# Zero-padded heads: score products of 64-column heads made 128 rows deep, and zero rows in DRAM written later

## Chip, cores and metric

The kernel runs on one core of one Trainium2 chip, in one launch. The metric is the time of one execution in microseconds on the device. The core has TensorE (PE in the rows; PEld is its weight load), VectorE (DVE), ScalarE (ACT), GpSimd (POOL) and SyncE (SP, which here only issues transfers).

## What is computed

Two blocks of a transformer on 512 tokens of width 1024, all in float32. The parts that the change touches are three attentions whose heads have 64 columns:

```python
# block 1, second attention (8 heads of 64, the selected keys only)
s = jnp.einsum('bqhd,bqkhd->bhqk', qi, k_sel) * (DSA_HEAD_DIM ** -0.5)
p = jax.nn.softmax(jnp.where(sel_ok[:, None], s, NEG), axis=-1)
# block 2, stick-breaking attention (8 heads of 64)
z = jnp.einsum('bhqd,bhkd->bhqk', q_blk, k) * dh ** -0.5
log_keep = jnp.where(past, jax.nn.log_sigmoid(-z), 0.0)
between = lax.cumsum(log_keep, axis=3, reverse=True) - log_keep
a = jnp.where(past, jnp.exp(jax.nn.log_sigmoid(z) + between), 0.0)
# block 2, dilated mixture (12 heads of 64 in three groups, dilations 1, 4, 16)
s = jnp.einsum('brhnqd,brhnkd->brhnqk', qs, kc) * dh ** -0.5
```

Between them stand a first attention in block 1 with 96 columns a head, a mixture of 32 experts, a memory attention with 128 columns a head in block 2, and at the end a layer that gathers rows of two tables of 16,384 experts.

## The kernel before

Every float32 product is made of three: each operand is split into a high part (a rounded copy, fp32r) and a low part (what is left), and `mm3` (lines 178 to 180) adds high x high, high x low and low x high into one PSUM bank. `split` (lines 185 and 187, or 188 and 189 with a scale) makes the parts: ScalarE casts the high one, VectorE (or GpSimd, where a weight is split for it) subtracts for the low one. Weights come in units of up to 512 KB through a ring of buffers `wr` and are split into `wh` and `wl`.

The block starts with the norm of four tiles of 128 tokens (`norm_T`): ScalarE sums squares, VectorE makes the root (`rs_v`, `rs_t`, `rs_y`) and the scaled tile `ny`, TensorE transposes it (line 271) and `split` writes it into HT and LT. Then the projection with `w1a` in four units, whose products (128x360) need all of that, and the next one with `w1b`. In this place GpSimd also zeroes a tile `zr` and writes it to DRAM with eight transfers: seven into `xs`, where the expert stage scatters tokens to later, and one into the last rows of `ys`.

A score product takes the features of one head from the rows of a tile: two heads of 64 columns stand above one another in 128 rows, and the product slices 64 of them (`rows`, `bs`). Between these products TensorE does other work, to keep it busy while the other engines do softmax: `fill` steps, products of the gates and output projections with 128 rows, transpositions of probabilities, and products with the values. A scheduler sets the order of the instructions on each engine from the program's dependencies and its own estimates, so code in another place or with other dependencies moves rows elsewhere.

In the stick-breaking stage each step (`logits`) copies scores z to u, makes az on VectorE, ScalarE, ScalarE, VectorE and GpSimd, and splits it into sp; `weights`, two steps later, adds products of sp with a triangle and makes the weights `at`. There are three buffers for az and four for u. In the dilated stage a step makes three products: s1 with 512 columns and two with 128.

The products of the memory attention (`mkT`, `mqT`) and of the index scores (`kiT`, already zero-padded per head) have 128 rows; those of the first attention (`kT`, `qT`) have 96.

Of the kernel before, what the change touches and what calls it, by code (L numbers as in the profile page):

```python
# [145 lines left out]
class Kernel:  # L146
# [233 lines left out]
    def block1_mix(self, cx, cm):  # L380
        nc, a = self.nc, self.a
        with ExitStack() as c0:
# [30 lines left out]
            with ExitStack() as c2:  # L413
# [29 lines left out]
                zr = pi.tile([P, XW // 7], F32, name="zr")  # L443
                nc.gpsimd.memset(zr, 0.0)
                for g in range(1, 8):
                    nc.gpsimd.dma_start(self.xs[g * P:(g + 1) * P].rearrange("p (r n) -> p r n", r=7),
                                      zr[:, None, :].to_broadcast([P, 7, XW // 7]))
                nc.gpsimd.dma_start(self.ys[896:1024].rearrange("p (r n) -> p r n", r=8),
                                  zr[:, None, 0:D // 8].to_broadcast([P, 8, D // 8]))
# [78 lines left out]
            with ExitStack() as c2:  # L528
# [31 lines left out]
            with ExitStack() as c2:  # L560
                pd = self.pool(c2, "b1d")
                qbT = [pd.tile([P, 4, 512], F32R, name=f"qbT{i}") for i in range(2)]
                kbT = [pd.tile([P, 4, 512], F32R, name=f"kbT{i}") for i in range(2)]
                vb = [pd.tile([P, NT, 512], F32R, name=f"vb{i}") for i in range(2)]
                hv = lambda x: x.rearrange("p (h r) -> p h r", h=8)
                for j, (dst, scale) in enumerate(((qbT, 0.125), (kbT, None))):
# [7 lines left out]
                    for jj in range(4):  # L574
                        self.transp([tok[:, t, jj * P:(jj + 1) * P] for t in range(NT)], P, dst[0][:, jj], dst[1][:, jj],
                                    scale=scale)
# [628 lines left out]
    def stick_qk(self, HT, LT, pool, half):  # L1205
        qT = [pool.tile([P, 2, 512], F32R, name=f"sqT{i}", tag=f"sqT{i}", bufs=1) for i in range(2)]
        kT = [pool.tile([P, 2, 512], F32R, name=f"skT{i}", tag=f"skT{i}", bufs=1) for i in range(2)]
# [10 lines left out]
    def stick(self, HT, LT, pq, qk, oT, fill):  # L1218

        nc = self.nc  # L1220
        with ExitStack() as c:
            pk = self.pool(c, "b2s")
            qT, kT = qk
            neg = pk.tile([P, P], F32, name="neg")
# [5 lines left out]
            nc.vector.tensor_copy(tri[1], neg)  # L1230
            self.tc.keep_in_program_order(nc.scalar.preload_act_table_set("natural_log_exp_and_others"))
            for half in range(2):
# [4 lines left out]
                self.stick_heads(pk, qT, kT, v, tri, oT[:, 2 * half:2 * half + 2], fill, half)  # L1237

    def stick_heads(self, pk, qT, kT, v, tri, oT, fill, half):
        nc = self.nc  # L1240
        sp, at = {}, {}

        def logits(i):
# [624 lines left out]
```

## Time and profile before

| | us |
|---|---|
| median of 3 runs | 2795.93 |
| lowest, highest | 2793.38, 2797.89 |
| the profiled execution | 2794.61 |
| its span, first to last instruction | 2792.6 |
| TensorE busy | 2674.3 (96%) |
| VectorE, ScalarE, GpSimd busy | 2066.8, 1290.4, 767.4 |

The granted clock of TensorE was 0.985 of full speed in the mean. Busy time of TensorE is from start to modelled end, so durations of neighbours overlap; how long a product holds the engine is read from the start of the next one. A row of the order of time gives start, duration, engine, line and operands; `64*128 64x256` is a stationary tile of 64 rows and 128 columns and a moving one of 64 rows and 256 columns. In brackets stands how long the engine had been idle, and what ended that.

### The profile page before, as it was taken

To read this page: it belongs to the slowest core of one execution; us is meant where nothing else is said; L and a number is where in the kernel's file an instruction comes from. 1 tells how busy PE (TensorE), PEld (TensorE's weight loads), DVE (VectorE), ACT (ScalarE), POOL (GpSimd) and SP (SyncE) were. 2 spreads that over 40 slices of the span, in tenths; PEclk is the share of its full clock that TensorE was granted. 3 is DMA by queue.
4 is the path that set the end of the run, shared out by engine and by line. 5 is a ranking of instruction groups with operands and counts; after the bars stand their busy time and mean duration, and the time that the engine had idled before them with its cause. 6 is when DMAs were issued, how large, how long until landed. Compare 5 with 4: busy or idle time off the path is not lost. (4 is left out here: it accounts for less than half of the span.)

```text
span 2792.6 us, 38328 instructions
## 1 busy us (share of the span) xinstructions
PE 2674.3 (96%) x13674; PEld 2296.3 (82%) x13674; DVE 2066.8 (74%) x4037; ACT 1290.4 (46%) x2029; POOL 767.4 (27%) x530
## 2 busy tenths in 40 slices
PE   6999999899999999899998999999999999999999
PEld 5887777677777878798877898999988888888887
DVE  4758856699988464654574898988778888778887
ACT  3544443577766564643433233355653333333332
POOL 1121110000001232210213351210125666665662
PEclk9999999999999999899999999999999999999999
DMA  7222228599984332231533246777678999999996
GB/s 190 78 69 80 83 84 300 197 344 354 355 306 125 110 106 85 72 98 61 170 132 134 77 139 196 229 252 255 247 281 317 342 355 357 348 347 338 347 338 231
DMA packets 231381, 595.69 MB, mean 213 GB/s; under 512 B 26128, under 2 KB 94992, under 8 KB 229520
## 3 DMA queue, kind: packets, MB, share of 16 engines
q1 hardware_dynamic: 192016, 450.52, 46.8%
q0 software_dynamic: 39168, 142.65, 14.4%
q8 instruction: 110, 1.80, 0.3%
q14 instruction: 87, 0.71, 0.1%
HBM read 524.91 MB, written 68.19 MB: 212 GB/s over the span
## 5 line engine op out<-in xcount | busy, mean ns | idle before, releaser
L185 ACT CAST wh<-wr 128x1024 fp32r<-128x1024 f32 (+3 forms) x637 | 621.4, 991 | 564.0 <-PE acc L179 226.9
L187 DVE TENSOR_TENSOR wl<-wr,wh 128x1024 fp32r<-128x1024 f32 (+3 forms) x483 | 574.7, 1204 | 143.1 <-ACT wh L185 141.7
L187 POOL TENSOR_TENSOR wl<-wr,wh 128x1024 fp32r<-128x1024 f32 (+1 forms) x154 | 318.9, 2080 | 777.1 <-ACT wh L185 738.3
L1576 POOL DMA_INDIRECT wr<-in_peer_u,idx x128 | 174.9, 1366 | 445.0 <-DVE dot L1581 204.8
L180 PE MATMUL acc<-hp,wl 128*128 128x384 f32 (+1 forms) x816 | 287.7, 353 | 7.6 <-DVE wl L187 7.6
L178 PE MATMUL acc<-hp,wh 128*128 128x384 f32 (+1 forms) x816 | 286.4, 352 | 0.0
L179 PE MATMUL acc<-hp,wh 128*128 128x384 f32 (+1 forms) x816 | 285.3, 350 | 0.0
L1576 POOL DMA_INDIRECT wr<-in_peer_v,idx x128 | 186.1, 1454 | 154.6 <-DVE x L1579 66.4
L185 ACT CAST WH<-act 128x384 fp32r<-128x384 f32 x128 | 65.9, 515 | 321.5 <-PE s L179 312.7
L1579 DVE SCALAR_TENSOR_TENSOR x<-wr,dot,x 128x1024 f32<-128x1024 f32 x128 | 195.2, 1525 | 18.2 <-DMA wr<-in_peer_v,idx 17.4
L1581 DVE CUSTOM_DVE_ANT_0 hy<-wr,gbc 128x1024 f32<-128x1024 f32 x128 | 173.0, 1352 | 39.9 <-DMA wr<-in_peer_u,idx 39.3
L178 PE MATMUL acc<-wh,WH 128*128 128x512 f32 x512 | 198.4, 392 | 3.9 <-ACT WH L185 3.9
L179 PE MATMUL acc<-wl,WH 128*128 128x512 f32 x512 | 200.9, 392 | 0.8 <-DVE wl L187 0.6
L180 PE MATMUL acc<-wh,WL 128*128 128x512 f32 x512 | 198.6, 389 | 0.0
L180 PEld LDWEIGHTS acc<-hp,wl 128*128 128x128 f32 x816 | 154.6, 190 | 16.2 <-DVE wl L187 11.1
L179 PEld LDWEIGHTS acc<-hp,wh 128*128 128x128 f32 x816 | 154.4, 189 | 5.3
L178 PEld LDWEIGHTS acc<-hp,wh 128*128 128x128 f32 x816 | 154.7, 190 | 4.8
L178 PEld LDWEIGHTS acc<-wh,WH 128*128 128x128 f32 x512 | 96.6, 189 | 23.0 <-ACT WH L185 4.2
L179 PEld LDWEIGHTS acc<-wl,WH 128*128 128x128 f32 x512 | 96.7, 189 | 20.9 <-DVE wl L187 2.4
L180 PEld LDWEIGHTS acc<-wh,WL 128*128 128x128 f32 x512 | 96.3, 188 | 20.3
L179 PE MATMUL s<-wl,XT 128*128 128x512 f32 x256 | 104.6, 409 | 5.4 <-DVE wl L187 5.3
L187 DVE TENSOR_TENSOR WL<-act,WH 128x384 fp32r<-128x384 f32 x128 | 78.0, 611 | 42.7 <-ACT WH L185 42.3
(650 smaller groups left out, 6885.7 us busy)
## 6 DMA issues: line engine op xcount, KB each, us to landing
wr<-in_peer_vL SPq DMA_DIRECT2D x128, 512.0 KB, 6.1
wr<-in_peer_uT SPq DMA_DIRECT2D x126, 512.0 KB, 4.8
wr<-in_w_gu SPq DMA_DIRECT2D x122, 512.0 KB, 5.3
wr<-in_w_dn SPq DMA_DIRECT2D x62, 512.0 KB, 5.3
gd<-stg SPq DMA_DIRECT2D x12, 2048.0 KB, 8.7
G<-gd SPq DMA_DIRECT2D x32, 768.0 KB, 11.2
act<-ad SPq DMA_DIRECT2D x72, 192.0 KB, 7.9
ad<-act SPq DMA_DIRECT2D x70, 192.0 KB, 4.1
```

Of the source, the lines that this page charges most:

```text
L178: mm(out, lh, rh, start=start, stop=False)
L179: mm(out, lh, rl, start=False, stop=False)
L180: return mm(out, ll, rh, start=False, stop=stop)
L185: nc.scalar.copy(H, src)
L187: return (le or nc.vector).tensor_tensor(L, src, H.bitcast(F32), op=ALU.subtract)
L1576: nc.gpsimd.indirect_dma_start(out=row, out_offset=None, in_=a["peer_u" if f == "dot" else "peer_v"], in_offset=bass.IndirectOffsetOnAxis( ...
L1579: nc.vector.scalar_tensor_tensor(x[:, 0], row, dot0[:, e:e + 1], x[:, 0], op0=ALU.mult, op1=ALU.add)
L1581: nc.vector.tensor_tensor_reduce(scr, row, h0, 1.0, 0.0, ALU.mult, ALU.add, accum_out=dot0[:, e:e + 1])
```

## The change

Four edits. The zero writes to `xs` and `ys` move from the first projection to the start of the first attention, behind the last weights fetched until then. In the second attention the keys are kept whole as float32 in `kb`, and `qk(h)` splits the 64 rows of one head into its half of `kbT`, a tile whose other rows are zero; there are two, for even and odd heads. The queries keep both heads in 128 rows, and the zero rows take the other head's part out. The stick-breaking stage does the same with `sk` and `skT` (`keys(h)`), and has two buffers for az in place of three. In the dilated stage it is the queries that are padded: `qT` holds them whole, and `queries(i)` splits 64 rows x 3 groups x 128 for a step into one of four tiles `dq`.

```diff
-                zr = pi.tile([P, XW // 7], F32, name="zr")
-                nc.gpsimd.memset(zr, 0.0)
-                for g in range(1, 8):
-                    nc.gpsimd.dma_start(self.xs[g * P:(g + 1) * P].rearrange("p (r n) -> p r n", r=7),
...
+                zr = pa.tile([P, XW // 7], F32, name="zr")
+                nc.gpsimd.memset(zr, 0.0)
+                rows = [(self.xs[g * P:(g + 1) * P], 7, XW // 7) for g in range(1, 8)] + [(self.ys[896:1024], 8, D // 8)]
+                for dst, r, n in rows:
+                    d = nc.gpsimd.dma_start(dst.rearrange("p (r n) -> p r n", r=r), zr[:, None, 0:n].to_broadcast([P, r, n]))
+                    self.after(d, self.loaded, "behind the weights")
...
-                kbT = [pd.tile([P, 4, 512], F32R, name=f"kbT{i}") for i in range(2)]
+                kb = pd.tile([P, 4, 512], F32, name="kb")
+                kbT = self.heads(pd, "kbT", 1)
...
+                            for t in range(NT):
+                                self.T(pt[:, t * P:(t + 1) * P], src[t])
+                            nc.scalar.copy(kb[:, jj], pt)
...
                 def qk(h):
-                    bs = slice((h % 2) * 64, (h % 2) * 64 + 64)
-                    return [x[bs, h // 2] for x in qbT], [x[bs, h // 2] for x in kbT]
+                    r = slice(64 * (h % 2), 64 * (h % 2) + 64)
+                    self.split(*[x[r, h % 2] for x in kbT], kb[r, h // 2])
+                    return [x[:, h // 2] for x in qbT], [x[:, h % 2] for x in kbT]
...
-                self.split(kT[0][:, cc - 2], kT[1][:, cc - 2], ps)
+                self.nc.scalar.copy(kT[:, cc - 2], ps)
...
+            kp = self.heads(pk, "skT", 1)
...
+        def keys(h):
+            r = slice(64 * (h % 2), 64 * (h % 2) + 64)
+            self.split(*[x[r, h % 2] for x in kp], kT[r, h // 2])
+
+        keys(0)
...
+            if i % NT == 1 and h < 3:
+                keys(h + 1)
...
-            ins = self.mm3(z[:, :n], kT[0][rows, h // 2, ks], kT[1][rows, h // 2, ks], qT[0][rows, h // 2, qs],
-                           qT[1][rows, h // 2, qs], True, True)
+            ins = self.mm3(z[:, :n], kp[0][:, h % 2, ks], kp[1][:, h % 2, ks], qT[0][:, h // 2, qs], qT[1][:, h // 2, qs],
+                           True, True)
...
-            az = pk.tile([P, 512], F32, name="az", tag="az", bufs=3)
+            az = pk.tile([P, 512], F32, name="az", tag="az", bufs=2)
...
+                def queries(i):
+                    hh, r = i // 4, i % 4
+                    rows = slice(64 * hh, 64 * hh + 64)
+                    self.split(*[x[rows] for x in qp[hh][r % 2]], qT[rows, :, r * P:(r + 1) * P])
...
+                    if i < 7:
+                        queries(i + 1)
+                    q = lambda g: [x[:, g] for x in qp[hh][r % 2]]
+                    k = lambda g, s: [x[:, g, s] for x in kT]
...
+    def heads(self, pool, name, n):
+
+        K = [pool.tile([P, 2 * n, 512], F32R, name=f"{name}{i}", tag=f"{name}{i}", bufs=1) for i in range(2)]
+        for x in K:
+            v = x.rearrange("p (n h) t -> p n h t", h=2).bitcast(F32)
+            self.nc.gpsimd.memset(v[64:128, :, 0], 0.0)
+            self.nc.gpsimd.memset(v[0:64, :, 1], 0.0)
+        return K
```

GpSimd's order from the end of the zero fills at the start to the splits for the first attention (`wl` are low parts of the gates' weights, `kT` the rotated key columns of the first attention), before:

```order
L426 MEMSET pe_243 128x4x64
L444 MEMSET zr 128x147
L446 DMA xs<-zr 896x1x147 x7
L448 DMA ys<-zr 1024x1x128
L187 TENSOR_TENSOR wl<-wr,wh 128x1024 x3
L533 CAST kT_1360<-peT_237 32x512
```

and with the change, in the same place:

```order
L426 MEMSET pe_243 128x4x64
L187 TENSOR_TENSOR wl<-wr,wh 128x1024 x3
L526 CAST kT_1350<-peT_237 32x512
L526 CAST kT_1351<-peT_238 32x512
L526 CAST kT_1352<-peT_237 32x512
L526 CAST kT_1353<-peT_238 32x512
L529 MEMSET zr 128x147
L532 DMA xs<-zr 896x1x147 x7
L532 DMA ys<-zr 1024x1x128
L187 TENSOR_TENSOR wl<-wr,wh 128x1024 x9
```

The zero writes stand behind three weight splits and the four key copies now, and ahead of the weight splits for the rest of that attention.

ScalarE's order around the keys of the second attention (`t` is the bank with the transposed keys, `vb` the values), before:

```order
L185 CAST kbT_2770<-t 128x512 x2
L185 CAST wh<-wr 128x1024
L185 CAST kbT_2770<-t 128x512 x2
L185 CAST oaH<-oaT 128x512 x4
L185 CAST wh<-wr 128x1024
L185 CAST vb_2772<-acc 128x512 x4
L185 CAST wh<-wr 128x1024
```

and with the change, on ScalarE in the same place (`kb` holds the whole keys):

```order
L583 COPY kb<-t 128x512 x2
L185 CAST kbT_2771<-kb 64x512 x2
L185 CAST wh<-wr 128x1024
L583 COPY kb<-t 128x512 x2
L185 CAST oaH<-oaT 128x512 x4
L185 CAST wh<-wr 128x1024
L185 CAST vb_2777<-acc 128x512 x4
L185 CAST wh<-wr 128x1024
```

The whole keys are copied in the same place, and the first two heads are split there; the other six casts of 64x512 stand further down, one among the softmaxes of each head.

TensorE's order where the stick-breaking stage begins (`mPT` and `Pr` belong to the memory attention, `wh,HTb` with 256 columns to the projection of the values `sv`), before:

```order
L271 MATMUL t<-ident,Pr 128x128 x2
L178 MATMUL s<-sqT_9304,skT_9306 128x128
L179 MATMUL s<-sqT_9305,skT_9306 128x128
L180 MATMUL s<-sqT_9304,skT_9307 128x128
L178 MATMUL s<-sqT_9304,skT_9306 128x256
L179 MATMUL s<-sqT_9305,skT_9306 128x256
L180 MATMUL s<-sqT_9304,skT_9307 128x256
L271 MATMUL t<-ident,Pr 128x128 x2
L178 MATMUL acc<-mPT_9923,mv_9035 128x512
L178 MATMUL acc<-wh,HTb 128x256
L179 MATMUL acc<-wl,HTb 128x256
```

and with the change, behind that projection (`oH,wh` is a fill product):

```order
L178 MATMUL acc<-wh,HTb 128x256
L179 MATMUL acc<-wl,HTb 128x256
L180 MATMUL acc<-wh,LTb 128x256
L178 MATMUL s<-sqT_9321,skT_10107 128x128
L179 MATMUL s<-sqT_9322,skT_10107 128x128
L180 MATMUL s<-sqT_9321,skT_10108 128x128
L178 MATMUL acc<-oH,wh 128x512
L179 MATMUL acc<-oH,wh 128x512
L180 MATMUL acc<-oH,wl 128x512
L178 MATMUL acc<-oH,wh 128x512
L179 MATMUL acc<-oH,wh 128x512
L180 MATMUL acc<-oH,wl 128x512
```

The first two score products of the stage stood ahead of the projection of the values and stand behind it now, with two fill steps behind each.

## Rows read from the trace of the kernel before

**Rows 1.** Stretch, length, us busy PE, PEld, DVE, ACT, POOL; granted clock, DMA, GB/s.

```profile
6.00:46.80 40.80, 21.17 (x104) 18.84 (x105) 18.26 (x52) 11.59 (x20) 6.17 (x7) 1.00 1.01 237
296.00:425.00 129.00, 127.46 (x611) 96.33 (x609) 84.97 (x255) 60.54 (x138) 20.10 (x11) 1.00 0.28 96
975.00:1175.00 200.00, 188.94 (x958) 152.78 (x957) 114.44 (x213) 116.01 (x258) 57.46 (x90) 0.97 0.27 85
1206.00:1425.00 219.00, 215.30 (x1200) 185.97 (x1200) 118.63 (x238) 94.44 (x170) 44.07 (x32) 0.98 0.39 126
```

**Rows 2.** Order of time, all engines, the start.

```profile
4.17 7.10 POOL L446 DMA_DIRECT2D xs<-zr  x7 [0.32 <-POOL zr L444]
4.64 4.54 SPq L196 DMA_DIRECT2D wr<-in_w1a  x4
7.89 1.28 DVE L333 SCALAR_TENSOR_TENSOR ny<-xt,rs_y,gbc 128x1024 f32<-128x1024 f32 x1
...
28.39 0.79 ACT L185 CAST wh<-wr 128x720 fp32r<-128x720 f32 x1 [10.03 <-DMA wr<-in_w1a]
...
29.24 1.15 PE L178 MATMUL acc<-wh,HT 128*128 128x360 f32 x2 [8.98 <-ACT wh L185]
...
51.53 0.47 PE L178 MATMUL acc<-wh,HT 128*128 128x512 f32 x1 [0.59 <-ACT scr L304]
```

**Rows 3.** Transfers issued in 0 to 45 us: KB each, median us to landing.

```profile
xs<-zr POOLq DMA_DIRECT2D x7, 514.5 KB, 20.2
...
wr<-in_w1b SPq DMA_DIRECT2D x4, 512.0 KB, 12.5
wr<-in_w1a SPq DMA_DIRECT2D x4, 360.0 KB, 28.1
```

**Rows 4.** Order of time, GpSimd, the first attention.

```profile
147.29 2.39 POOL L187 TENSOR_TENSOR wl<-wr,wh 128x1024 fp32r<-128x1024 f32 x1 [17.48 <-ACT wh L185]
```

**Rows 5.** Order of time, TensorE, one score product of the stick-breaking stage.

```profile
1004.18 0.40 PE L180 MATMUL acc<-oH,wl 128*128 128x512 f32 x1
1004.50 0.38 PE L178 MATMUL s<-sqT,skT 64*128 64x256 f32 x1
1004.73 0.28 PE L179 MATMUL s<-sqT,skT 64*128 64x256 f32 x1
1004.85 0.28 PE L180 MATMUL s<-sqT,skT 64*128 64x256 f32 x1
1005.06 0.50 PE L178 MATMUL acc<-oH,wh 128*128 128x512 f32 x1
1005.39 0.40 PE L179 MATMUL acc<-oH,wh 128*128 128x512 f32 x1
```

**Rows 6.** Order of time, TensorE, one score product of the memory attention.

```profile
926.99 0.39 PE L180 MATMUL acc<-HTb,wl 128*128 128x512 f32 x1
927.22 0.28 PE L178 MATMUL s<-mkT,mqT 128*128 128x256 f32 x1
927.34 0.28 PE L179 MATMUL s<-mkT,mqT 128*128 128x256 f32 x1
927.46 0.28 PE L180 MATMUL s<-mkT,mqT 128*128 128x256 f32 x1
```

**Rows 7.** Instructions that touch qbT, sqT and dqT: ns min/median/max, first and last start.

```profile
L178 PE MATMUL s<-kbT,qbT x32: 323/384/498, 313.5 to 418.6; 64*128 64x128 f32 x8, 64*128 64x256 f32 x8, 64*128 64x384 f32 x8, 64*128 64x512 f32 x8
...
L178 PE MATMUL s<-sqT,skT x32: 322/410/501, 979.1 to 1151.9; 64*128 64x128 f32 x8, 64*128 64x256 f32 x8, 64*128 64x384 f32 x8, 64*128 64x512 f32 x8
...
L178 PE MATMUL s<-dkT,dqT x48: 217/324/501, 1232.1 to 1409.9; 64*128 64x128 f32 x32, 64*128 64x512 f32 x16
```

**Rows 8.** Order of time, TensorE, a wait in the stick-breaking stage.

```profile
1029.42 0.38 PE L1272 MATMUL t<-sp,tri 128*128 128x256 f32 x1 [1.78 <-ACT sp L185]
```

**Rows 9.** Instructions that touch kT (first attention): splits of 64x512.

```profile
L185 ACT CAST kT<-s x8: 578/580/582, 136.6 to 226.4; 64x512 fp32r<-64x512 f32 x8
L187 DVE TENSOR_TENSOR kT<-s,kT x8: 672/679/684, 137.2 to 227.3; 64x512 fp32r<-64x512 f32 x8
```

More of the change, by code (lines that the diff above doesn't have):

```diff
@@ L1206, in stick_qk @@
         qT = [pool.tile([P, 2, 512], F32R, name=f"sqT{i}", tag=f"sqT{i}", bufs=1) for i in range(2)]
-        kT = [pool.tile([P, 2, 512], F32R, name=f"skT{i}", tag=f"skT{i}", bufs=1) for i in range(2)]
+        kT = pool.tile([P, 2, 512], F32, name="sk", tag="sk", bufs=1)
         def ev_qk(cc, ps):
@@ L1223, in stick @@
             qT, kT = qk
-            neg = pk.tile([P, P], F32, name="neg")
+            neg = pk.tile([P, 512], F32, name="neg", tag="az", bufs=2)[:, :P]
             tri = [pk.tile([P, P], F32R, name=f"tri{i}") for i in range(2)]
@@ L1322, in dilated @@
                     copy(X[:, k:k + 2].rearrange("p k (r l) -> p k r l", r=4), w.rearrange("p k (l r) -> p k r l", r=4))
+            qp = [[[pd.tile([P, 3, P], F32R, name=f"dq{h}{b}{i}", tag=f"dq{h}{b}{i}", bufs=1) for i in range(2)]
+                   for b in range(2)] for h in range(2)]
+            for h in range(2):
+                for b in range(2):
+                    for x in qp[h][b]:
+                        nc.gpsimd.memset(x[64 - 64 * h:128 - 64 * h].bitcast(F32), 0.0)
             for half in range(2):
@@ L1330, in dilated @@
                     self.head_norm(pd, tok, 6, 64)
-                for nm, gg in (("q", gq), ("k", gk)):
-                    tok = qk[nm]
-                    T = [pd.tile([P, 3, 512], F32R, name=f"d{nm}T{i}", tag=f"d{nm}T{i}", bufs=1) for i in range(2)]
-                    for g in range(3):
-                        self.transp([tok[:, t, g * P:(g + 1) * P] for t in range(NT)], P, T[0][:, g], T[1][:, g], scale=gg)
-                    qk[nm] = T
+                pts = [self.bank(x) for x in "tts"]
+                for g in range(3):
+                    for t in range(NT):
+                        self.T(pts[g][:, t * P:(t + 1) * P], qk["q"][:, t, g * P:(g + 1) * P])
+                qT = pd.tile([P, 3, 512], F32, name="dqT", tag="dtok", bufs=1)
+                for g in range(3):
+                    nc.scalar.activation(qT[:, g], pts[g], AF.Copy, scale=gq)
+                tok = qk["k"]
+                kT = [pd.tile([P, 3, 512], F32R, name=f"dkT{i}", tag=f"dkT{i}", bufs=1) for i in range(2)]
+                for g in range(3):
+                    self.transp([tok[:, t, g * P:(g + 1) * P] for t in range(NT)], P, kT[0][:, g], kT[1][:, g], scale=gk)
                 v = [pd.tile([P, NT, 384], F32R, name=f"dv{i}", tag=f"dv{i}", bufs=1) for i in range(2)]
@@ L1344, in scores @@
                     j = 2 * half + hh
-                    rows = slice(64 * hh, 64 * hh + 64)
                     rs = slice(r * P, (r + 1) * P)
-                    q = lambda g: [x[rows, g, rs] for x in qk["q"]]
-                    k = lambda g, s: [x[rows, g, s] for x in qk["k"]]
+                    if i < 7:
+                        queries(i + 1)
+                    q = lambda g: [x[:, g] for x in qp[hh][r % 2]]
+                    k = lambda g, s: [x[:, g, s] for x in kT]
                     s1, s2 = self.bank("s"), self.bank("s")
```

18 lines of the change are left out of this document (9 added, 9 removed).

## The prediction

> **What bounds the kernel now.** I read the busy times by stretch first, then the instructions in order of time where the change works. In the second attention of block 1 TensorE is busy for 127.46 us of 129, in the stick-breaking stage for 188.94 of 200, in the dilated stage for 215.30 of 219; VectorE and ScalarE have 34% to 57% of each stretch idle [rows 1]. So in these stages a nanosecond taken from TensorE's own sequence is a nanosecond of the end, except where TensorE already waits for a chain of the others (11 us of the stick-breaking stretch). The start is different: TensorE does next to nothing until 29.24 us.
>
> **The start: eight zero writes leave it.** What holds TensorE at the start is one landing. The first weights are issued at 4.64 us, and ScalarE casts them at 28.39 us, having sat idle 10.03 us for that DMA; the first product follows at 29.24 us [rows 2]. In the first 45 us those four transfers of 360 KB take 28.1 us to land, beside seven zero writes of 514.5 KB that GpSimd issues from 4.17 us on and one of 512 KB; the next weights, which come behind, take 12.5 us [rows 3]. The zeros are needed only by the expert stage, hundreds of microseconds later.
>
> With them gone, what is late next is VectorE's chain of norms, low parts and weight splits. Between 6 us and the last split of these weights at 46.8 us VectorE works 18.26 us [rows 1]; packed without a gap it would end at 24.3 us, a gain of 22 us, but each tile's part waits for a transposition and a cast, and TensorE must still do its products. Bounds: if the stretch from the first product to the first of the next projection (29.24 to 51.53, 22.3 us [rows 2]) keeps its length, and the first product comes when the cast is free behind the first tiles, some 6 us after the first normalized tile at 7.89 us [rows 2], it starts at about 14 us and the gain is 15 us. If the weights still take the 12.5 us of the transfers behind [rows 3], they land at 4.64 + 12.5 = 17.1 us, the product starts at about 18 us, and the gain is 11 us. The upper end is 19 us, if VectorE packs better than now. I take **14 us**: TensorE is fully used for most of what follows, so the shift should last to the end.
>
> Where the zeros go: GpSimd now issues them behind the four key copies, right ahead of the weight split at 147.29 us, before which it sits idle for 17.48 us [rows 4]. The eight issues take 7.10 us for seven [rows 2] and I estimate another 2 to 3 us for the eighth, so they fit; behind them on GpSimd stands only that split. They pass three weight splits and the key copies, which nothing on GpSimd delays now. They also wait for the landing of the last weights fetched before, which the products ahead of the attention have used by then, so this wait is over when they come. If the cover were gone, the split would be late by at most those 10 us, once. The transfers themselves meet a stretch in which SyncE fetches weights ahead of their use; the landing of 20.2 us for a zero write [rows 3] would be seen only if the next fetch were due within that time. I cost this at nothing, at worst 5 us.
>
> **The 64-row products.** Around one score product of the stick-breaking stage, between products with 128 rows, I read starts, since durations overlap [rows 5]. The last 128-row product takes 0.32 us to the next start (1004.18 to 1004.50), the first 64-row one 0.23, the second 0.12, the third 0.21 until the 128-row product at 1005.06, and that one 0.33. The comparison is a score product with 128 rows and the same 256 columns in the memory attention, also between 512-column products: 0.23 us before it, then 0.12 and 0.12 [rows 6]. So two starts on the way in and two on the way out are late: 0.09 + 0.11 + 0.09 + 0.10 = **0.39 us** for each visit to the 64-row products. Within the visit nothing is lost, and the columns cost the same with 64 rows as with 128. So giving these products zero rows should take away the visit's price and add no TensorE time.
>
> A rule speaks against this. The Trainium skill (TensorE: Matmul & The Clock Gate, section Part 3: Packing small matmuls) says that products that use different row groups of the array run concurrently, which full rows would end. The rows show no such overlap: the first 64-row product is followed after 0.23 us, the second after 0.12, never sooner than with 128 rows [rows 5, 6]. By the rows nothing is lost; by the rule the sum is that of rival 3.
>
> How many visits: 32 products of three matmuls in the second attention, 32 in the stick-breaking stage, 48 in the dilated one (three at each of 16 steps) [rows 7]. Counted in the order of time, TensorE comes to a 64-row product from something else 33, 33 and 36 times, 102 in all; some products stand together, and some are broken up. About a quarter of the sides is a transposition, behind which another switch remains after the change, so I take 0.34 us a visit: 102 x 0.34 = 35 us. Bounds: 0.2 us (only the 64-row halves) gives 20 us, 0.39 gives 40 us.
>
> How much of it reaches the end: in the second attention (33 x 0.34 = 11 us) and in the dilated stage (12 us) TensorE has no idle time to speak of, so I take 10.5 and **11**. In the stick-breaking stage (11 us) it waits already, for 1.78 us at one place [rows 8], for the chain of az, sp and u; a faster TensorE waits more there. I take **7**, between 0 and 11. Together 28.5 us.
>
> **What the change adds.** Second attention: the keys are copied whole (four copies in place of four casts of the same size) and then split per head: eight more casts of 64x512 on ScalarE at 0.580 us and eight low parts at 0.679 in place of four on VectorE [rows 9]: 4.6 and at most 3 us over 129 us, of which ScalarE has 68 idle [rows 1]. ScalarE casts head h+1 while head h's products run, so the next head does not wait. The stick-breaking stage gets the same eight splits, on ScalarE with 116.01 us busy in 200 [rows 1]. The dilated stage gets 16 splits of 64x384, which cannot cost more than a 64x512 one: under 10 and 11 us, on engines with 125 and 100 us idle [rows 1]; six whole splits turn into six scalings. Two steps' queries alternate between buffers, so a split waits only for the step before the last. The zero fills on GpSimd come once per stage and lie in its idle time. Two az buffers in place of three: counted in VectorE's order, only five of 32 steps opened one while two others were open, so I cost this at nothing in the middle and let it take the 7 us at worst. On TensorE the first stick-breaking product moves behind the projection of the values; the work before and after it is the same, so I cost this at nothing too, with the fill products as cover.
>
> **Sum.** The profiled execution took 2794.61 us (span 2792.6 and 2.0 around it), 1.3 below the median of the runs shown. 2794.6 - 14 - 28.5 = 2752.1, so I predict **2752 us**.
>
> **Rivals.**
> 1. *Only part of it arrives* (2765 to 2785). VectorE's chain keeps the start at its low bound (11 us), the stick-breaking stage gives nothing because its chain sets the pace, and the other two stages turn a third of their saving into waits for VectorE: 11 + 0 + 14 = 25, so 2770 us. For it: the wait of 1.78 us, and that VectorE has 85 us of work in the 129 of the attention [rows 1]. Against it: TensorE's idle time in two of three stages is under 4 us.
> 2. *The stick-breaking chain becomes the bound* (slower). Place: az with two buffers and the key split ahead of each head's first product, on ScalarE. If every one of the 32 steps had the wait that one step shows today, 1.78 us [rows 8], it would cost 57 us against 35.5 saved elsewhere (14 + 10.5 + 11): 2816 us. It decides from 1.1 us a step on. Against it: ScalarE and VectorE are idle for more than 40% of the stretch.
> 3. *The zero rows cost what idle array rows gave.* If 64-row products of different heads ran side by side in the array, filling the rows would end that. The products' columns (8 heads x 3 x 1280 twice, and 16 x 3 x 768, 98,000 columns at 0.12 us for 256) take 46 us; half of that lost, and only the start gained, gives 2794.6 - 14 + 23 = 2804 us. Against it: the spacing of rows 5 and 6, and that neighbouring products are mostly of one head, so of one half of the rows.
> 4. *The switch is not the tiling* but something of score products as such; then only the start gains: 2781 us. The memory attention's products, which come between the same neighbours without it, speak against it [rows 6]. The Trainium skill (TensorEngine Tiling (Array Packing), section Key Properties) says that a change of tiling mode drains the engine; that is the forecast's cause, and leaves this rival little.
>
> **Numbers.** Forecast (2738 to 2762) 0.62; rivals 1 and 4 (2762 to 2785) 0.27 and 0.03; more than 56 us gained 0.02; rivals 2 and 3 0.03 and 0.01; no change 0.02. The range of 8 in 10 adds the low bounds: start 10, attention 6, stick-breaking 0, dilated 6, so 22 us: 2773; and the high ones, 17 + 11 + 11 + 13 = 52, and 1 to 4 for gaps closed elsewhere at the start: 2739. A measurement of this kernel tells 0.2% (about 6 us) from no change: faster 0.94, within it 0.02, slower 0.04.
>
> **What would show it.** Right: no product with 64 rows in the trace; the spacing at a stick-breaking product 0.23, 0.12, 0.12, 0.12, 0.23; the first product before 18 us and the first of the next projection before 40; the zero writes after 100 us with no wait of TensorE behind them; the stretches of rows 1 shorter by about 10, 7 and 11 us. Wrong: the first weights cast early but the next projection later than 42 us (VectorE's chain); TensorE's idle time in the stick-breaking stretch up from 11 to 20 us or more, with waits for sp or u; the starts around score products still 0.3 us apart.

## The result and the profile after

Over five runs each, the changed kernel takes 2768.37 us in the median (2763.64 to 2771.37), the kernel before 2795.93 (2793.38 to 2802.51): a ratio of 0.9895, interval 0.9883 to 0.9906. A second set (after_again, below) gave 2771.4 against 2799.18, ratio 0.9903 (0.9879 to 0.9926). So it is faster by about 28 us, 1%, where 43 were forecast. The profiled execution took 2771.37 us, the slowest of its five; span 2769.7, granted clock 0.983 in the mean.

The page of the changed kernel, busy time by engine:

```profile
PE 2645.3 (96%) x13674; PEld 2299.1 (83%) x13674; DVE 2084.7 (75%) x4055; ACT 1303.8 (47%) x2061; POOL 775.3 (28%) x546
```

TensorE lost 29 us of work against the table of before, VectorE gained 18 and ScalarE 13 (the splits per head), GpSimd 8.

The order of time of the changed kernel, the start and the zero writes, which answers to [rows 2, 4]:

```profile
4.74 3.80 SPq L196 DMA_DIRECT2D wr<-in_w1a  x4
...
12.79 2.19 ACT L185 CAST wh<-wr 128x720 fp32r<-128x720 f32 x3
...
14.41 0.65 PE L178 MATMUL acc<-wh,HT 128*128 128x360 f32 x1
...
37.43 0.47 PE L178 MATMUL acc<-wh,HT 128*128 128x512 f32 x1 [2.66 <-DVE wi L440]
...
120.70 7.09 POOL L532 DMA_DIRECT2D xs<-zr  x7 [0.35 <-POOL zr L529]
126.08 2.61 POOL L532 DMA_DIRECT2D ys<-zr  x1
133.81 2.39 POOL L187 TENSOR_TENSOR wl<-wr,wh 128x1024 fp32r<-128x1024 f32 x1 [5.12 <-ACT wh L185]
```

The first weights are issued when they were, but cast at 12.79 us and no longer at 28.39. The first product starts at 14.41 us, the next projection at 37.43 in place of 51.53: 14.1 us earlier, behind a new wait of 2.66 us for VectorE. The zero writes stand at 120.7 to 128.7 us, and the split behind them comes 13.5 us before its old place, as everything around it does. It waits 5.12 us for ScalarE's cast after the zero writes have ended, and TensorE's waits around there add up to 6.6 us (6.7 before), so the zero writes delay nothing that the trace shows.

Three stretches of both kernels, cut at the same instructions (from the first transposition of qktok to the first product of ob; from the first 256-column product of the projection of the values to the first 384-column one of the dilated stage; from there to the last product of PA). Columns as in [rows 1]; first the kernel before:

```profile
278.32:429.15 150.83, 147.10 (x707) 112.65 (x705) 105.80 (x294) 69.37 (x150) 20.88 (x12) 1.00 0.29 97
981.48:1177.16 195.68, 183.15 (x928) 148.29 (x926) 114.23 (x209) 114.91 (x252) 55.51 (x89) 0.96 0.28 90
1177.16:1423.93 246.77, 243.07 (x1340) 213.74 (x1341) 133.84 (x269) 112.27 (x190) 44.07 (x32) 0.97 0.38 122
```

The same of the changed kernel:

```profile
265.36:405.92 140.56, 136.53 (x708) 113.84 (x706) 109.75 (x299) 73.98 (x159) 19.93 (x12) 0.99 0.31 105
961.16:1160.28 199.12, 179.10 (x934) 153.26 (x933) 123.16 (x215) 119.11 (x260) 62.88 (x101) 0.94 0.27 88
1160.28:1395.34 235.06, 229.27 (x1340) 212.00 (x1341) 140.37 (x279) 118.44 (x206) 42.69 (x32) 0.99 0.40 128
```

The first and the third shrink by 10.3 and 11.7 us. TensorE's busy time falls by as much or more (10.6 and 13.8 us; in the third its idle time grows by 2.1). The second grows by 3.4 us although TensorE's busy time in it falls by 4: its idle time (length less busy) went from 12.5 to 20.0 us, and its granted clock from 0.96 to 0.94. Elsewhere the profiled pair agrees but for drift: 2.9 us are lost between the two blocks' attentions and 5.7 behind the dilated stage, where both kernels have the same instructions but for the copies of the stick-breaking keys, in part in another order. 13.0 won up to the second attention, 10.3 in it, 2.9 and 3.4 lost, 11.7 won, 5.7 lost: but for rounding 22.9, the difference of the spans.

One score product of the stick-breaking stage in the changed kernel, TensorE in order of time, which answers to [rows 5]:

```profile
975.33 0.40 PE L180 MATMUL acc<-oH,wl 128*128 128x512 f32 x1
975.57 0.28 PE L178 MATMUL s<-sqT,skT 128*128 128x256 f32 x1
975.69 0.28 PE L179 MATMUL s<-sqT,skT 128*128 128x256 f32 x1
975.80 0.28 PE L180 MATMUL s<-sqT,skT 128*128 128x256 f32 x1
975.92 0.39 PE L178 MATMUL acc<-oH,wh 128*128 128x512 f32 x1
976.15 0.39 PE L179 MATMUL acc<-oH,wh 128*128 128x512 f32 x1
```

The starts are 0.24, 0.12, 0.11, 0.12 and 0.23 us apart, as in the memory attention [rows 6]: the 0.39 us of a visit are gone, and no product with 64 rows is left in the trace.

What TensorE waited for in the stick-breaking stage: releaser, us in total, times, longest. First the kernel before:

```profile
PE t L1272 <- ACT sp L185: 2.9, 2, 1.8
PE t L1272 <- DVE sp L187: 2.8, 4, 1.5
PE s L178 <- ACT u L1254: 1.3, 1, 1.3
PE acc L178 <- ACT at L185: 1.1, 2, 0.8
```

And the changed kernel:

```profile
PE t L1288 <- ACT sp L185: 5.7, 3, 2.4
PE acc L178 <- ACT at L185: 4.6, 2, 3.6
PE t L1288 <- DVE sp L187: 2.8, 4, 2.1
PE t L1288 <- DVE u L1294: 2.3, 2, 1.4
```

The waits are for the same chain as before, sp, u and at: 15.4 us in these rows in place of 8.1. Another 4.3 us of the stage's idle time is one wait for HTb right ahead of the dilated stage, the same in both kernels. So the question for the experiments is why the stick-breaking stage kept nothing of its saving.

### The profile page after: what moved, and what is told of

The parts are those of the page before. It is cut to its first block, busy times and chain, and to the rows that moved or that the text cites. A ratio compares the mean times of both kernels' runs of the same rounds, so it can differ in the third digit from the quotient of the medians.

```text
span 2769.7 us, 38424 instructions
## 1 busy us (share of the span) xinstructions
PE 2645.3 (96%) x13674; PEld 2299.1 (83%) x13674; DVE 2084.7 (75%) x4055; ACT 1303.8 (47%) x2061; POOL 775.3 (28%) x546
## 5 line engine op out<-in xcount | busy, mean ns | idle before, releaser
L180 PE MATMUL acc<-hp,wl 128*128 128x384 f32 (+1 forms) x816 | 287.2, 353 | 10.3 <-DVE wl L187 10.3
L1616 DVE SCALAR_TENSOR_TENSOR x<-wr,dot,x 128x1024 f32<-128x1024 f32 x128 | 196.7, 1537 | 21.1 <-DMA wr<-in_peer_v,idx 20.2
```

Of the source, the lines that this page charges most:

```text
L180: return mm(out, ll, rh, start=False, stop=stop)
L1616: nc.vector.scalar_tensor_tensor(x[:, 0], row, dot0[:, e:e + 1], x[:, 0], op0=ALU.mult, op1=ALU.add)
```

## The experiments

Times are medians of four to six runs, ratios are to runs of the kernel before on the same chip. A stage is measured in the profiled execution between the landmarks of the second stretch above. Two columns of the table further down are worked out: "idle" is length less busy; "clock" is an estimate of what the lower level cost: the stage is cut into 40 equal slices, and each slice's length times (1 less its granted clock) is added up. Waits that fall into the lower level are counted in it too, 0.2 to 2.7 us by execution.

**zeros_only**: the kernel before with the zero writes moved, nothing else.

```diff
-                zr = pi.tile([P, XW // 7], F32, name="zr")
...
+                zr = pa.tile([P, XW // 7], F32, name="zr")
...
+                    self.after(d, self.loaded, "behind the weights")
```

> Before, with the zero writes moved and nothing else. Theory (the start is worth what its landmarks show, the first product of the second projection 14.1 us earlier, 13.0 us left at the first attention): 2795.9 - 13 = 2783 us, and the first product of the second projection near 37.4 us. Rival (an earlier start is eaten by the weight stream of the experts, which comes no sooner): under 5 us, 2791 us or more.

2784.66 us, ratio 0.9958 (0.9944 to 0.9972): some 11.7 us. In its trace the next projection starts 13.1 us earlier than before, the first attention 14.1, the memory attention 12.5, the end 10.2. The start's term is right, and it lasts but for drift.

**dilated_old**: the changed kernel with the dilated stage as before.

```diff
-                    self.split(*[x[rows] for x in qp[hh][r % 2]], qT[rows, :, r * P:(r + 1) * P])
...
-                    q = lambda g: [x[:, g] for x in qp[hh][r % 2]]
+                    q = lambda g: [x[rows, g, rs] for x in qk["q"]]
```

> The changed kernel with the dilated stage as before. Theory (36 visits at 0.34 us, all on the path, as the landmarks show: 11.7 us): the stage is 11 to 12 us longer than in the changed kernel, 2780 us. Rival (the stage got shorter by the new order of the transpositions and the scalings without splits, not by the spacing): less than half of that, 2774 us or less.

2777.76 us, ratio 0.994 (0.9923 to 0.9957). The dilated stage takes 245.4 us (235.1 with padded queries): the padding gives 10.3 us there, in its own stage, as forecast. The edit also takes back the new order of the transpositions and the scalings; the starts tell the two apart. Each time from one start of TensorE to the next, less the wait in it and multiplied by its granted clock, was added up over the stage: beside a score product these times are 37.2 us in dilated_old and 25.5 in the changed kernel, everywhere else 199.8 and 200.2. So it is the spacing of the score products, and not the new order.

The trace of dilated_old shows something else too. The order of TensorE's instructions is the same as in the changed kernel until behind the stick-breaking stage, and yet that stage is 5 us shorter. The windows of dilated_old, the stick-breaking stage:

```profile
961.80:1155.90 194.10, 174.24 (x935) 148.66 (x933) 122.99 (x215) 118.93 (x260) 58.41 (x93) 0.96 0.28 90
```

The idle time is that of the changed kernel (19.9 us against 20.0), the busy time 4.9 us less. The order of time, TensorE, behind the first long wait, in the changed kernel:

```profile
987.98 0.45 PE L1288 MATMUL t<-sp,tri 128*128 128x384 f32 x1 [2.32 <-ACT sp L185]
...
992.29 0.63 PE L178 MATMUL acc<-oH,wh 128*128 128x512 f32 x1
992.72 0.63 PE L179 MATMUL acc<-oH,wh 128*128 128x512 f32 x1
993.15 0.63 PE L180 MATMUL acc<-oH,wl 128*128 128x512 f32 x1
```

and in dilated_old, the same instructions:

```profile
988.61 0.44 PE L1288 MATMUL t<-sp,tri 128*128 128x384 f32 x1 [2.31 <-ACT sp L185]
...
992.06 0.40 PE L178 MATMUL acc<-oH,wh 128*128 128x512 f32 x1
992.29 0.39 PE L179 MATMUL acc<-oH,wh 128*128 128x512 f32 x1
992.52 0.40 PE L180 MATMUL acc<-oH,wl 128*128 128x512 f32 x1
```

The same wait of 2.3 us; behind it the products start 0.43 us apart in one execution (granted clock 0.50 in these rows, the level of 1.2 GHz) and 0.23 in the other (1.00, that of 2.4 GHz). So this wait cost its own length in both executions and, in one of them, a stretch at half the clock besides.

**after_again**: the changed kernel, unaltered, for a third execution of that order.

> The changed kernel, unaltered. Two profiled executions of the same order of the stick-breaking stage (the changed kernel's, and that of dilated_old, which differs only behind it) took 199.1 and 194.1 us, with TensorE idle 20.0 and 19.9 us in both. Theory D: the stage's length is set by how much of it TensorE stands at the lower granted clock behind its waits, and that falls differently in each execution; a third execution has the same waits (idle 19 to 21 us) and a stage anywhere from 194 to 200 us, by the granted clock (0.94 to 0.96). Rival: 194.1 came from something in the dilated stage's code, and this one shows 199 again within 0.5 us.

2771.4 us, ratio 0.9903 (0.9879 to 0.9926). The windows of this execution, the stick-breaking and the dilated stage:

```profile
965.07:1160.04 194.97, 175.38 (x935) 149.94 (x933) 123.19 (x215) 119.02 (x260) 61.93 (x101) 0.95 0.28 90
1160.04:1394.31 234.27, 228.93 (x1341) 211.66 (x1341) 140.36 (x279) 118.76 (x206) 43.76 (x32) 0.99 0.39 127
```

Idle 19.6 us, length 195.0: theory D holds. One order of instructions gave 199.1, 194.1 and 195.0 us with the same waits. So a stage's length is compared over several executions here, and idle time, which repeats within 0.4 us, tells more than length.

**stick_old**: the changed kernel with the stick-breaking stage as before (64-row products, three az buffers).

```diff
-            ins = self.mm3(z[:, :n], kp[0][:, h % 2, ks], kp[1][:, h % 2, ks], qT[0][:, h // 2, qs], qT[1][:, h // 2, qs],
...
+            ins = self.mm3(z[:, :n], kT[0][rows, h // 2, ks], kT[1][rows, h // 2, ks], qT[0][rows, h // 2, qs],
...
-            az = pk.tile([P, 512], F32, name="az", tag="az", bufs=2)
+            az = pk.tile([P, 512], F32, name="az", tag="az", bufs=3)
```

> The changed kernel with the stick-breaking stage as before (64-row score products, three az buffers, no key splits). Theory (padding made this stage slower: its landmarks lost 3.4 us where 7 were forecast as gain): 2768.4 - 3 = 2765 us. Rival (the 3.4 us are the later start of the first two score products alone, which this moves back too, and the stage is even otherwise): the same 2765, but with the second half of the stage as long as in the changed kernel. Prediction as it stood (the stage saves 7 us): 2775 us.

2761.40 us, ratio 0.9876 (0.9861 to 0.989), below the changed kernel's 2768 and 2771, and not the 2775 of the prediction as it stood. Its stage:

```profile
958.06:1154.78 196.72, 184.91 (x929) 149.52 (x927) 114.03 (x209) 114.86 (x252) 59.84 (x97) 0.95 0.28 89
```

Idle 11.8 us, but a length in the middle of the three of the changed kernel. So the padding neither shortens nor lengthens this stage measurably. The 7 and 10 us between the whole times are not all the stage's: when the memory attention begins, ahead of any difference in TensorE's order, stick_old stood 23.4 us before the kernel before, the changed kernel 20.3 and after_again 16.4.

**stick_old_az2**: stick_old with two az buffers.

```diff
-            az = pk.tile([P, 512], F32, name="az", tag="az", bufs=3)
+            az = pk.tile([P, 512], F32, name="az", tag="az", bufs=2)
```

> As stick_old, with two az buffers in place of three. Theory A (the third az buffer is what the stage lost): the stage gets some 8 us longer than in stick_old, 2773 us, with TensorE waiting for sp. Theory B (the stage is bound by the chain of the other engines, or the key splits lengthen it): within 2 us of stick_old.

2762.65 us, ratio 0.9885 (0.987 to 0.9899), 1.3 us above stick_old and inside its interval. Its stage:

```profile
957.92:1156.81 198.89, 183.88 (x929) 148.22 (x927) 115.35 (x209) 114.46 (x252) 59.48 (x97) 0.96 0.26 88
```

Idle 15.0 us: the third buffer is worth 3.2 us of waits against stick_old, and 2.1 and 2.5 against the other two executions with three buffers (12.9 in zeros_only, 12.5 before), even with the slower products. The stage is 2.2 us longer, far from the 8 of theory A. So the buffer accounts for less than half of the 7.4 us by which the changed kernel's idle time grew (means of three executions each, below).

**stick_az_by_block**: the changed kernel with an az and a u buffer for each of the four key blocks, each as wide as its block (less memory than two and four of 512).

```diff
-            az = pk.tile([P, 512], F32, name="az", tag="az", bufs=2)
-            u = pk.tile([P, 512], F32, name="u", tag="u", bufs=4)
+            az = pk.tile([P, n], F32, name="az", tag=f"az{kt}", bufs=1)
+            u = pk.tile([P, n], F32, name="u", tag=f"u{kt}", bufs=1)
```

> The changed kernel with az and u in one buffer for each of the four key blocks, of the block's own width: u has four buffers in turn as before, az four in place of two, in 2 KB less. Theory A (az buffers): the stage gives the 7 us that were forecast, 2768.4 - 8 to 10 = 2759 us. Theory B (chain or key splits): within 2 us of the changed kernel, 2768 us.

2760.24 us, ratio 0.9874 (0.9858 to 0.9889). Its stage:

```profile
959.09:1153.90 194.81, 177.58 (x935) 151.80 (x933) 120.79 (x215) 119.13 (x260) 63.65 (x101) 0.95 0.28 90
```

Idle 17.2 us, 2.4 to 2.8 less than in the changed kernel, which agrees with the 2.1 to 3.2 of stick_old_az2. The other 4.8 us of new waits stay. The stage is as long as in dilated_old and after_again, so the lower whole time is not shown to come from it.

Three more edits of this kernel looked for those 4.8 us.

**az_block_half_keys**: of the four key splits of each half two are left out, so that the last two heads of a half are scored against the keys of the first two.

```diff
-            if i % NT == 1 and h < 3:
+            if i % NT == 1 and h < 1:
```

> As stick_az_by_block, without the key splits of the last two heads of each half (their products take the keys of the first two heads): four of the eight splits are left out. Theory C (the key splits on ScalarE and VectorE lengthen the chain): the stage, 194.8 us from the projection of the values to the dilated stage, gets 2 to 5 us shorter. Theory B (what is left of the lost gain is the chain's latency, in which TensorE waits and falls to the low clock): within 1 us of 194.8.

2758.02 us, ratio 0.9863 (0.9846 to 0.9879). Its stage:

```profile
960.55:1150.32 189.77, 173.01 (x935) 148.36 (x933) 114.68 (x211) 116.38 (x256) 62.30 (x101) 0.97 0.29 92
```

5.0 us shorter, which looks like theory C; but the idle time is 16.8 us, only 0.4 less, and the granted clock 0.97 against 0.95. By the table below 5.0 us is what the clock gave, and one order of instructions differed by 4.6 us in that column between executions. Half of the key splits cost 0.4 us of waits, no more than idle time differs between executions of one order; as far as waits go, costing them at nothing was right.

**az_block_lag3**: weights follow logits by three steps in place of two.

```diff
-LG = [1, 1, 2, 1]
+LG = [1, 1, 3, 1]
```

> As stick_az_by_block, with the weights of a step three steps behind its scores in place of two. Theory B (latency of the chain): TensorE's waits for sp in the stage fall from 16.9 us to under 10 and the stage gets 5 us or more shorter, 2755 us. Theory C (work of ScalarE and VectorE, not latency): no change within 2 us, 2760 us, or longer where u is reused sooner.

2762.40 us, ratio 0.989 (0.987 to 0.991); stage 198.4, idle 20.1. The 16.9 us that the expectation puts to sp are all of TensorE's waits in this stretch of stick_az_by_block; those for sp are 10.4 us of them, and 8.9 here. In their place stand 4.9 us for `at`, and ScalarE's copy into u now waits three times for the last reader of that buffer (1.5 us). The shorter stage that theory B forecast did not come. But u had no more buffers than before, so the edit does not show that the chain's length is without effect.

**az_block_pool_lows**: the low parts of the keys on GpSimd.

```diff
-            self.split(*[x[r, h % 2] for x in kp], kT[r, h // 2])
+            self.split(*[x[r, h % 2] for x in kp], kT[r, h // 2], le=nc.gpsimd)
```

> As stick_az_by_block, with the low parts of the keys made by GpSimd in place of VectorE (0.7 us each taken off VectorE, over 1 us each put on GpSimd, which is busy 64 us of 195 and makes az and u too). Theory C: 2 us or more shorter. Theory B: within 1 us, or longer by the waits for GpSimd.

2765.09 us, ratio 0.9885 (0.9868 to 0.9902); stage 198.3, idle 21.3. Idle is 4.1 us more than in stick_az_by_block, as theory B had it: GpSimd makes the selects on az and u, and TensorE's waits for u went from 2.2 to 5.8 us.

**scores_first** and **az_block_scores_first**: the first two steps' scores of each half are written ahead of the projection of the values, in the changed kernel and in stick_az_by_block.

```diff
+        first = [logits(0), logits(1)]
+        project()
-        staged(4 * NT, LG[2], logits, weights)
+        staged(4 * NT, LG[2], lambda i: first[i] if i < 2 else logits(i), weights)
```

> The changed kernel with the first two steps' score products of each half of the stick-breaking stage written ahead of the projection of the values, so that the chain of u, az and sp starts under that projection. Theory S: the waits came from the late start, since the first score products moved behind the projection; with the chain started earlier TensorE's idle time between the memory attention's last score product and the dilated stage's first product falls from 20 to 13 us or less, and the whole takes 2761 us or less. Rival A (two az buffers and a chain that is no shorter): the waits stay (idle 17 us or more), some 2766 to 2770 us.

> As scores_first, with one az and one u buffer per key block (the edit of stick_az_by_block) as well. If both the late start and the two az buffers cost something, the stage is shorter than with either edit, idle time 10 us or less, and the whole takes 2753 to 2757 us. If the chain's own length sets the pace, the time stays at that of stick_az_by_block, 2760 us within 2, with 15 us idle or more.

2769.57 us, ratio 0.9902 (0.9876 to 0.9927), and 2763.28 us, ratio 0.987 (0.9843 to 0.9897). From the memory attention's last score product to the dilated stage TensorE idles 18.9 us in both, where the three executions of the changed kernel have 21.8, 21.6 and 21.3 and stick_az_by_block has 19.0. So the later start of the chain costs 2 to 3 us of waits in the changed kernel, not the 7 or more of theory S, and it does not add to the buffers' share: the two edits together take off no more waits than either. The median of scores_first stays at that of the changed kernel, though its profiled execution took 2756.72 us, the shortest of its five.

**stick_fill_lows_dve**: the longest wait of the changed kernel between the score products of this stage (3.63 us for `at`) has a cause outside the chain's own work. The order of time around it, TensorE's products left out but the last:

```profile
1009.36 2.85 POOL L187 TENSOR_TENSOR wl<-wr,wh 128x512 fp32r<-128x512 f32 x2 [1.11 <-ACT wh L185]
...
1011.00 1.62 DVE L1271 SCALAR_TENSOR_TENSOR az<-u 128x384 f32<-128x384 f32 x1
...
1012.17 1.15 POOL L1295 TENSOR_SCALAR_AFFINE_SELECT u<-u 128x128 f32<-128x128 f32 x3
...
1012.66 0.52 ACT L1272 ACTIVATE az<-az 128x384 f32<-128x384 f32 x1 [2.18 <-DVE az L1271]
...
1013.64 1.12 ACT L1297 ACTIVATE u<-u 128x512 f32<-128x512 f32 x3
...
1014.67 0.80 ACT L185 CAST at<-u 128x512 fp32r<-128x512 f32 x2
1015.32 0.80 PE L178 MATMUL acc<-at,sv 128*128 128x512 f32 x1 [3.63 <-ACT at L185]
```

GpSimd makes low parts of a fill weight for 2.85 us; three selects on u queue behind them, VectorE's az beside them takes 1.62 us, ScalarE sits 2.18 us for that az with the exponentials of u behind it, and `at` is late. The edit puts the 24 low parts on VectorE.

```diff
-            self.nxt = [0, self.k.wunit(j[0], 8, P, le=self.k.nc.gpsimd, cut=self.cut), j, None]
+            self.nxt = [0, self.k.wunit(j[0], 8, P, le=self.le or self.k.nc.gpsimd, cut=self.cut), j, None]
...
+            fill.le = nc.vector
             self.stick(HT, LT, pq, sqk, osb, fill)
+            fill.le = None
```

> The changed kernel with the 24 low parts of the fill steps' weights in the stick-breaking stage made on VectorE and no longer on GpSimd. In the changed kernel's trace the stage's longest wait (3.63 us for at) follows two of these low parts in a row on GpSimd (2.85 us) with the three selects on u queued behind them, and VectorE's az over 384 columns beside them took 1.62 us where the median is 0.49 to 0.56. Theory G: these splits are a main part of the chain's length; without them TensorE's idle time in the stage falls from 20 us (19.6 to 20.0 in three executions) to 14 or less, the stage is 188 to 192 us, the whole 2760 to 2764. Rival: the low parts only move onto VectorE (24 x 0.69 = 17 us more there, in the same chain); idle time stays at 18 us or more and the whole within 2 us of 2768 to 2771.

2762.23 us, ratio 0.9877 (0.9848 to 0.9906), which looks like theory G; but the stage takes 195.8 us, and its idle time is 18.7. In the stage the rival holds: that wait is gone, and others of up to 3.2 us for sp take its place. The lower whole time comes from other stretches.

The traces tell more of these slow steps than the one wait. In the changed kernel 14 of VectorE's steps on az, u and sp in the stage take over 0.3 us longer than the shortest of their line and shape, 13.6 us in sum, each of them while GpSimd makes a low part of a weight. In stick_old there are 9 (6.8 us), in stick_old_az2 10 (8.3), in stick_az_by_block 14 (11.8), and in this run none. So the chain's own work is longer in the changed kernel than with the old products. This run takes the slow steps away but puts 24 low parts on VectorE instead, in the same chain. Two others tell more: against stick_az_by_block the slow steps fall to 7.5 us in az_block_half_keys and to 6.7 in az_block_scores_first, and the idle time by 0.4 and 0.1 us. So they are no large part of the new waits.

The stick-breaking stage of all kernels with the same landmarks, in us:

| kernel | length | idle | clock | busy less clock |
|---|---|---|---|---|
| before | 195.7 | 12.5 | 7.5 | 175.7 |
| zeros_only | 197.2 | 12.9 | 6.8 | 177.5 |
| stick_old | 196.7 | 11.8 | 9.1 | 175.8 |
| stick_old_az2 | 198.9 | 15.0 | 8.6 | 175.3 |
| after | 199.1 | 20.0 | 11.9 | 167.2 |
| dilated_old | 194.1 | 19.9 | 7.3 | 167.0 |
| after_again | 195.0 | 19.6 | 9.0 | 166.4 |
| stick_az_by_block | 194.8 | 17.2 | 10.3 | 167.3 |
| az_block_half_keys | 189.8 | 16.8 | 5.3 | 167.7 |
| az_block_lag3 | 198.4 | 20.1 | 12.2 | 166.1 |
| az_block_pool_lows | 198.3 | 21.3 | 11.3 | 165.6 |
| stick_fill_lows_dve | 195.8 | 18.7 | 12.8 | 164.3 |

The last column sorts the kernels by their score products alone: 175.3 to 177.5 with 64 rows, 164.3 to 167.7 with 128. Idle and clock take back what that column gives. (In the kernels with 64 rows two of the 32 score products stand ahead of this stretch. Cut from the memory attention's last score product on, where all have the same work, the means of the next section come out as 10.6 us from the products, 8.4 of new waits and 1.7 of clock, and the same 0.5 us won.)

## Why the prediction was right, and where a term was mis-sized

The measured 2768 us lies inside the stated range (2739 to 2773), but not in the forecast's own band (2738 to 2762): it lies in that of rival 1, which had a chance of 0.27. Of the four terms three came near their forecast. In the profiled pair 22.9 us were won where 42.5 were added up; of the 19.6 missing, 10.4 are the stick-breaking stage's (3.4 lost, 7 forecast) and 8.6 come from stretches that the prediction did not price.

**The start (14 us): right.** The first product came at 14.41 us, the next projection 14.1 us earlier, and zeros_only has 13.1 to 14.1 of it by itself. The next thing late was VectorE's chain, as forecast, with a wait of 2.66 us. The zero writes' new place cost nothing that shows.

**The price of a visit and two of three stages: right.** The second attention gave 10.3 us (forecast 10.5), the dilated stage 11.7 in the profiled pair and 10.3 by dilated_old (forecast 11). Over 33 and 36 visits that is 0.31 us and 0.29 to 0.33 us each, for 0.34. It repeats: the stretch of the second attention takes 150.8 and 152.3 us in the two kernels with 64-row keys and 140.4 to 141.0 in the twelve others, and the dilated stage 245.4 to 247.7 in the three with 64-row queries and 234.1 to 237.5 in the eleven others. Rivals 3 and 4 are out: the spacing of filled products is that of [rows 6], and stages shrink where the rows are filled. The Trainium skill (TensorEngine Tiling (Array Packing), section Key Properties) says that a change of tiling mode drains TensorE; the trace agrees that a change costs time, about 0.3 us for a visit.

**The stick-breaking stage (7 us): mis-sized.** The step that failed is "a faster TensorE waits more there. I take 7, between 0 and 11", with "Two az buffers in place of three: counted in VectorE's order, only five of 32 steps opened one while two others were open, so I cost this at nothing in the middle", and of the first product's move behind the projection "I cost this at nothing too". It measured +3.4 in the profiled pair. Over executions, the means of three with the old scores and three az buffers (before, zeros_only, stick_old) and of three of the changed order (after, dilated_old, after_again) are 196.5 and 196.1 us: some 0.5 gained, nothing beside the 5 us by which one order differs. By the columns: the products give 9.4 us (176.3 to 166.9, or 0.28 us for each of 33 visits), new waits take 7.4 (12.4 to 19.8), and the lower clock 1.6 (7.8 to 9.4), which is inside the spread of that column.

Of the new waits 2.6 go with the third az buffer (12.4 to 15.0 in stick_old_az2, and again 19.8 to 17.2 in stick_az_by_block). The other 4.8 (15.0 to 19.8) come with the padded products as the change has them: faster products, the key splits, and the later start of the first two. Half the key splits are worth 0.4 us. Starting the chain earlier removes 2 to 3 us in the changed kernel, but none beside the buffers. A longer lag does not remove the 4.8, and moving GpSimd's low parts to VectorE takes off 1.1. The slow steps on VectorE, 13.6 us in place of 6.8 to 8.3, are no large part either. What is left is that TensorE, with less work of its own, waits out the chain; that is argued, not shown, and the cause of the 4.8 us stays open to that extent.

This is the part of rival 1 that came about: the stage gives nothing, with waits for its chain. The rest of rival 1 did not: the start won more than 11 us, and the other two stages kept their saving. That the measured time stands beside its 2770 us is luck. Rival 2 has the mechanism but not the price: 7.4 us of waits over 32 steps are 0.23 us a step, far from the 1.1 from which it would decide. The prediction named the sign of it, idle time up from 11 to 20 us with waits for sp or u, and that is what the trace shows.

**The rest of the gap.** The profiled pair also lost 8.6 us in stretches where both kernels have the same instructions. Such stretches differ between executions of one kernel: the changed kernel stood 20.3, 19.7 (dilated_old, the same code until then) and 16.4 us before the kernel before when the memory attention began. Why the medians of stick_old, stick_az_by_block and stick_fill_lows_dve lie 6 to 11 us below the changed kernel's, when against the mean of its three executions their stages account for 1.3 at most, stays open. These medians come from several chips, on which the kernel before took 2795.93 to 2800.47 us; by the ratios the gap is 5 to 8 us (0.9874 to 0.9877 against 0.9895 and 0.9903). The prediction had no term for such stretches.

The lowest median with the whole computation is that of stick_az_by_block, 2760.24 us: its interval (0.9858 to 0.9889) lies below 1 and mostly below that of the changed kernel (0.9883 to 0.9906). stick_old's overlaps both. So no run shows that padding the stick-breaking stage is worth anything; the start, the second attention and the dilated stage carry the change.

## What to carry to other kernels

Read the price of a switch from the starts around the product, and count the visits in the order of time; where TensorE has no idle time, that product arrives (10 to 12 us of 11 here). Where the trace of before already shows TensorE waiting on a chain, saved TensorE time can turn into waits, as here, so price the stage by the chain, and price a removed buffer by taking it away alone in the old kernel (2 to 3 us here). Compare idle time, which repeated within 0.4 us, before stage lengths, which moved by 5 us between executions of one order.

## What the runs showed of the hardware

One order of instructions with the same waits within 0.4 us took 194.1, 195.0 and 199.1 us, by how long TensorE stood at 1.2 GHz behind those waits: 7.3, 9.0 and 11.9 us lost by the estimate of the table. The Trainium skill (TensorE: Matmul & The Clock Gate, Part 1: The HAM clock gate) calls the number of slow products at a kernel's start run-variable for one and the same kernel; these three executions show the same behind waits in the middle of one.

VectorE's az over 128x384 takes 0.55 to 0.64 us in eleven of 16 cases in the stick-breaking stage of the changed kernel, and 1.57 to 1.65 us in the five in which GpSimd makes low parts of a weight beside it:

```profile
979.90 0.56 DVE L1271 SCALAR_TENSOR_TENSOR az<-u 128x384 f32<-128x384 f32 x1
...
1119.35 1.57 DVE L1271 SCALAR_TENSOR_TENSOR az<-u 128x384 f32<-128x384 f32 x1
```

With those low parts on VectorE (stick_fill_lows_dve) all 16 take 0.54 to 0.65 us. That removed the wait shown above and left the stage's idle time at 18.7 us, with 24 low parts more on VectorE.
